# Where SP waits for the store: behind both closing barriers, on a semaphore that the closing clear does not touch

## The chip, the cores and the metric

One core of a Trainium2 chip. The metric is device microseconds of one execution; lower is better. The experiments ran on three chips, each beside the kernel before on the same chip. All runs in this text are fast: at full granted clock, and none over 1.5% above the fastest of its kernel. The core has five instruction queues: SP (issues most transfers here), ACT (ScalarE), DVE (VectorE), POOL (GpSimd) and PE (TensorE, which computes nothing in this kernel but takes part in every barrier).

A semaphore is a counter on which the queues wait for each other. Two kinds of instruction recur below: an EventSemaphore waits on a semaphore, changes it, or both; a DRAIN stands where a queue closes a piece of its work, and can wait on a semaphore and change one as well. In a barrier of the closing block every other queue counts itself in ("gather"), and goes on when POOL has seen all of them and counts up a second semaphore ("release").

"After the store's issue" below means: counted from the start of the last transfer that SP issues, the one that writes the result. Such times to the nanosecond are from the traces' records of instructions and of semaphore events; the printed views round to a tenth or a hundredth of a microsecond.

## The reference

```python
batch, dim = 1024, 4096          # x, y: float32
def reference(x, y, axis):       # axis = -1
    return np.sum(np.abs(x - y), axis=axis).astype(np.float32)
```

The kernel reads 33.5 MB and writes 4 KB.

## The kernel before

Each partition holds 8 rows. VectorE subtracts, ScalarE takes absolute values and sums, the last row goes in five pieces. What matters here is the end: the sums `ro` go out in one store, and SP's wait for that store is put ahead of the closing block which the framework adds to every kernel. In this cut, whose comments are added, `put` places an instruction in the program, and `s_end` counts the partial results.

```python
class Entry:
    ...
    def at_end(self, emit):
        nc = self.nc
        hook = nc.inst_callbacks[-1]
        here = nc.cur_bb.bb.name
        done = []

        def closing(ins):                    # called for each instruction that is added
            if done or nc.cur_bb.bb.name == here or ins.engine != mybir.EngineType.SP:
                return
            done.append(ins)
            emit()                           # at the first SP instruction of the closing block
        ...

    s_end = tc.alloc_semaphore("s_end")
    s_out = tc.alloc_semaphore("s_out")
    ...
    put(lambda: nc.sync.wait_ge(s_end, n_part + 3))
    put(lambda: nc.sync.dma_start(out=orr, in_=ro).then_inc(s_out, 16))
    entry.at_end(lambda: nc.sync.wait_ge(s_out, 16))
```

The closing block itself, as the built program has it (shortened: each barrier has a DRAIN and an EventSemaphore for each of PE, ACT, DVE and SP):

```
SP    DRAIN            waits for s_out (before the change)
each  DRAIN            joins barrier 1: counts up "gather"
POOL  EventSemaphore   waits for all of "gather";  POOL EventSemaphore: counts up "release"
each  EventSemaphore   waits for "release"
POOL  clears the range of semaphores 99 to 112 (the kernel's own)
each  DRAIN            joins barrier 2, and so on as in barrier 1
```

## Time and profile before

| | before |
|---|---|
| time, median of all 6 runs beside the changed kernel | 85.35 us |
| time of the profiled run | 85.36 us |
| its span (first to last instruction of the kernel) | 83.57 us |
| time less span | 1.79 us |
| store's issue starts | 81.346 us into the span |
| sixteenth increment of `s_out` | 1.447 us after it |
| SP's and PE's last instruction end | 2.180 and 2.225 us after it |

To read it: everything up to the store's issue is loads and arithmetic, and the change touches none of it. Left are 2.2 us of the span and 1.8 us outside the span (the records do not say how much of these lies ahead of the first instruction). The page's chain of waits does not show this part at all: it is followed back from the last instruction of a computing engine, and ends with VectorE's last sum at 81.32. Only the view of SP's own waits and the listing of the closing line's instructions do; the prediction shows both.

### The profile page before, as it was taken

The page shows a single profiled execution, that of the slowest core. Times are in us where ns is not written, and L with a number is a line of the kernel's source. Part 1 is how long each engine was busy: PE and PEld are TensorE (multiplying, and loading weights), DVE is VectorE, ACT ScalarE, POOL GpSimd, SP SyncE. Part 2 cuts the span into 40 slices and gives each one's busy share as a digit, 9 for nine tenths or more (in the row PEclk, how much of TensorE's full clock was granted, in tenths as well). Part 3 has the DMA queues.
Part 4 walks back from the last instruction along what each step waited for, and adds up shares of the span by engine and source line. Part 5 has one row for each costly group of instructions (what it writes and reads, how often), then busy time and mean ns, then how long its engine had stood idle before and what let it go on. Part 6 is the DMA issues. An engine that isn't in the chain of part 4 may idle for free.

```text
span 83.6 us, 103 instructions
## 1 busy us (share of the span) xinstructions
DVE 36.3 (43%) x16; ACT 31.6 (38%) x27; POOL 0.2 (0%) x4
## 2 busy tenths in 40 slices
DVE  0000000000000000000399999999099898997870
ACT  3200000000000000000002979697980899999960
POOL 0000000000000000000000000000000000000000
DMA  5991992992998899888889988889999999999910
GB/s 125 627 627 71 557 627 125 502 627 125 502 502 376 376 588 541 376 376 376 376 376 659 471 376 376 376 376 416 447 392 463 416 447 379 414 410 410 394 55 2
DMA packets 2592, 33.56 MB, mean 402 GB/s; under 512 B 416, under 2 KB 928, under 8 KB 1696
## 3 DMA queue, kind: packets, MB, share of 16 engines
q1 hardware_dynamic: 2448, 25.17, 71.6%
q10 hardware_dynamic: 144, 8.39, 23.2%
HBM read 33.55 MB, written 0.00 MB: 402 GB/s over the span
## 4 chain that ended last, share of the span: by engine, by line
DMA 68%; DVE 22%; ACT 7%; ACTq 0%; SPq 0%; issue 0%
DMA xa_rows<-in_x_dram 49%; DMA yb_rows<-in_y_dram 19%; DVE xa_rows L123 16%; ACT xb_rows L128 7%; DVE xb_rows L123 5%; DVE ro_sums L159 1%; ACTq L195 0%; SPq L102 0%
## 5 line engine op out<-in xcount | busy, mean ns | idle before, releaser
L123 DVE TENSOR_TENSOR xa_rows<-xa_rows,yb_rows 128x4096 f32<-128x4096 f32 x4 | 17.4, 4421 | 41.1 <-DMA xa_rows<-in_x_dram 41.1
L128 ACT ACTIVATE xa_rows<-xa_rows 128x4096 f32<-128x4096 f32 x4 | 14.5, 3617 | 44.9 <-DVE xa_rows L123 44.9
L123 DVE TENSOR_TENSOR xb_rows<-xb_rows,yb_rows 128x2048 f32<-128x2048 f32 (+5 forms) x9 | 17.9, 2019 | 3.6 <-DMA yb_rows<-in_y_dram 3.5
L128 ACT ACTIVATE xb_rows<-xb_rows 128x2048 f32<-128x2048 f32 (+5 forms) x9 | 15.2, 1686 | 3.1 <-DVE xb_rows L123 3.0
L128 ACT ACT_TABLE_LOAD x1 | 1.3, 1283 | 1.3 <-PEq L181 1.3
L128 ACT ACTIVATION_READ_ACCUMULATOR xb_rows<-xb_rows 128x1 f32 x9 | 1.7, 186 | 0.0
L128 ACT ACTIVATION_READ_ACCUMULATOR xa_rows<-xa_rows 128x1 f32 x4 | 0.7, 187 | 0.0
L157 DVE TENSOR_TENSOR last_piece<-xb_rows,yb_rows 128x288 f32<-128x288 f32 x1 | 0.5, 459 | 0.2 <-DMA yb_rows<-in_y_dram 0.2
L159 DVE TENSOR_REDUCE ro_sums<-last_piece 128x1 f32<-128x292 f32 x1 | 0.5, 458 | 0.1
L151 DVE TENSOR_REDUCE ro_sums<-half_sums 128x2 f32<-128x4 f32 x1 | 0.1, 149 | 0.0
L181 POOL MEMSET const-bfloat16-1.0<- 128x1 bf16 x1 | 0.1, 102 | 0.0
L181 POOL MEMSET const-uint8-127<- 128x1 uint8 x1 | 0.1, 102 | 0.0
L181 POOL MEMSET const-float32-1.0<- 128x1 f32 x1 | 0.1, 99 | 0.0
L181 POOL MEMSET const-float32-0.0<- 128x1 f32 x1 | 0.1, 98 | 0.2 <-issue 0.2
## 6 DMA issues: line engine op xcount, KB each, us to landing
xa_rows<-in_x_dram SPq DMA_DIRECT2D x1, 6144.0 KB, 40.6
xb_rows<-in_x_dram SPq DMA_DIRECT2D x1, 6144.0 KB, 54.3
yb_rows<-in_y_dram SPq DMA_DIRECT2D x3, 2048.0 KB, 15.5
xa_rows<-in_x_dram SPq DMA_DIRECT2D x1, 2048.0 KB, 24.1
xb_rows<-in_x_dram SPq DMA_DIRECT2D x1, 864.0 KB, 17.8
yb_rows<-in_y_dram SPq DMA_DIRECT2D x1, 864.0 KB, 16.0
xb_rows<-in_x_dram SPq DMA_DIRECT2D x1, 528.0 KB, 16.9
yb_rows<-in_y_dram SPq DMA_DIRECT2D x1, 528.0 KB, 17.7
```

Of the source, the lines that this page charges most:

```text
L123: put(lambda: nc.vector.tensor_sub(out=tx, in0=tx, in1=ty).then_inc(s_sub, 1))
L128: put(lambda: nc.scalar.activation(tx, tx, ABS, accum_out=to).then_inc(sem, 1))
L151: put(lambda: nc.vector.reduce_sum(out=ro[:, K - 3:K - 1], in_=half, axis=AX).then_inc(s_end, 1))
L157: put(lambda: nc.vector.tensor_sub(out=last[:, n_part:n_part + w], in0=tx, in1=ty).then_inc(s_end, 1))
L159: put(lambda: nc.vector.reduce_sum(out=ro[:, K - 1:K], in_=last, axis=AX, apply_absolute_value=True).then_inc(s_end, 1))
L181: nc = _bacc.Bacc("TRN2", target_bir_lowering=False, num_devices=1)
```

## The change

The intent: SP needs to hold the program open until the store has landed, but nobody else needs to wait for that. If SP waits behind the barriers, the barriers can run while the store is in flight. The first barrier is followed by POOL's clearing of the kernel's semaphores; a count that is still arriving must not be cleared, so `s_out` is now allocated outside of the kernel's range (the clear covers 99 to 111) and SP counts it back to zero itself.

```diff
-            if done or nc.cur_bb.bb.name == here or ins.engine != mybir.EngineType.SP:
+            if done or nc.cur_bb.bb.name == here or ins.engine != mybir.EngineType.Pool:
+                return
+            mine = [x.opcode for x in nc.cur_bb.bb.instructions if x.engine == mybir.EngineType.SP]
+            if mine.count("EventSemaphore") < 2:
                 return
...
-    s_out = tc.alloc_semaphore("s_out")
+    s_out = nc.alloc_semaphore("s_out")
...
-    entry.at_end(lambda: nc.sync.wait_ge(s_out, 16))
+    entry.at_end(lambda: nc.sync.wait_ge(s_out, 16).then_inc(s_out, -16))
```

In the built program this is one wait less on SP's first closing DRAIN (which stays) and one EventSemaphore more as SP's last instruction.

## The prediction

> **What bounds the kernel now.** All times below are microseconds from the span's start unless marked ns; starts to the nanosecond are from the trace's records of instructions and semaphore events, where the views round to a tenth.
>
> I read the page's head and its chain first, to see how much of the kernel the change can touch at all.
>
> ```profile
> span 83.6 us, 103 instructions
> DVE 36.3 (43%) x16; ACT 31.6 (38%) x27; POOL 0.2 (0%) x4
> DMA 68%; DVE 22%; ACT 7%; ACTq 0%; SPq 0%; issue 0%
> ```
>
> Two thirds of the chain are loads; no compute engine is busy half of the time. The body is bound by 33.55 MB at 402 GB/s and by the tail of the last pieces, and the change has no instruction there. It can only win after the last reduction. The timeline of the last microseconds shows where that begins:
>
> ```profile
> 80.86 0.46 DVE L159 TENSOR_REDUCE ro_sums<-last_piece 128x1 f32<-128x292 f32 x1
> 81.35 0.35 SPq L163 DMA_DIRECT2D out_dram<-ro_sums  x1
> ```
>
> The last sum ends at 81.32, SP issues the store from 81.346 to 81.693, and the span ends at 83.57. So 2.2 us of the span follow the store's issue start, with no engine computing. The view of what SP's queue waited for, from 82 to 84, says what fills them:
>
> ```profile
> SPq L195 <- DMA out_dram<-ro_sums: 1.1, 1, 1.1
> SPq L195 <- PEq L195: 0.6, 2, 0.4
> ```
>
> First a wait of 1.1 for the store, then two waits of together 0.6 inside the closing barriers. The first is a wait for memory, the second for the other engines, and before the change they come one after the other. The listing of the closing line's instructions has the pieces:
>
> ```profile
> L195 POOLq EVENT_SEMAPHORE  x4: 17/17/17, 82.9 to 83.5; - x4
> L195 SPq DRAIN  x3: 7/7/7, 82.8 to 83.1; - x3
> L195 SPq EVENT_SEMAPHORE  x2: 17/17/17, 83.0 to 83.5; - x2
> L195 PEldq EVENT_SEMAPHORE  x2: 51/51/51, 83.0 to 83.5; - x2
> L195 POOLq EVENT_SEMAPHORE_RANGE_CLEAR  x1: 114/114/114, 83.2 to 83.2; - x1
> ```
>
> SP's first DRAIN carries the wait for the store and starts at 82.809. Then: SP's DRAIN of the first barrier at 82.870, GpSimd collects at 82.903 and releases at 82.981, SP passes at 83.023; second barrier: SP's DRAIN at 83.114, GpSimd's DRAIN at 83.062, its clearing of the semaphores at 83.167 for 114 ns, DRAIN at 83.310, collecting at 83.389, release at 83.467; SP's last instruction at 83.509 (ends 83.526), PE's last at 83.520, 51 ns, which is the end at 83.571.
>
> **What the Trainium skill says.**
> "DMA: Bandwidth & Descriptors", section "Anatomy of one DMA — SWDGE (gpsimd) path": a DMA's semaphore cannot be updated until the last byte is confirmed to have landed, and HBM is the slowest target. The store here is issued by SP and not by GpSimd, but the trace agrees in kind: its packets are on the engines from 82.19 to 82.39, and its 16 increments come from 82.593 to 82.793. So 0.4 us of its flight is confirmation; nothing in the change shortens it.
>
> "Perfetto Trace Analysis", section "Sequencer-only Instruction (DRAIN, etc)": such an instruction is shown only from the moment its semaphores are satisfied to its end; its waiting and the propagation of its update are not shown. The trace agrees: the DRAIN that waited over a microsecond is 7 ns long, and starts 16 ns after the sixteenth increment. So the new last instruction will look short as well, and its start is what to read.
>
> "Runtime: NRT & Kernel Launch", section "The ~15µs preamble/postamble breakdown": after the kernel the runtime runs a barrier over all engines and then resets semaphores. Its section "Semaphores 0–2 are reserved" names semaphore 2 as that barrier's. The trace has events of semaphore 2 from 83.806 to 84.330, nine of them, and the profiled run's time is 85.36 against a span of 83.57: 1.79 us lie outside the span. That barrier needs SP too, so SP's exit still counts.
>
> **The change part by part.**
> Removed: the wait on SP's first DRAIN. The DRAIN itself stays, without a wait. Added: one EventSemaphore on SP behind its last barrier instruction, which waits for the 16 and takes 16 off. In the built program the listing of instructions is otherwise the same, and the range that GpSimd clears ends one semaphore earlier (99 to 111 in place of 99 to 112), so the closing barriers cannot wipe a count that is still arriving. Taking 16 off restores zero. Two costs need sizing: when SP now gets through the barriers, and what its last wait adds.
>
> 1. SP is free at 81.693, when the store's issue ends. What a DRAIN right behind a DMA issue costs can be read from the opening, where SP issues two loads and then meets the first barrier:
>
> ```profile
> L181 SPq DRAIN  x1: 125/125/125, 0.9 to 0.9; - x1
> ```
>
> That issue ended at 0.850 and the DRAIN started at 0.904, 54 ns later, and lasted 125 ns. So here: 81.693 + 0.054 + 0.125 = 81.872. In that opening case megabytes were in flight for tens of microseconds more, so a DRAIN does not wait for its engine's transfers to land.
>
> 2. The next DRAIN, the first barrier's: before, it started 82.870 - 82.816 = 0.054 after the end of the one ahead. So 81.872 + 0.054 = 81.926.
>
> 3. Both barriers: before, from SP's barrier DRAIN to the end of SP's last instruction 83.526 - 82.870 = 0.656, and to PE's end 83.571 - 82.870 = 0.701. All other engines were long in the barrier (ACT's and DVE's DRAINs end at 80.86 and 81.37), so SP is the one it waits for and the same length applies: SP through at 82.582, PE at 82.627.
>
> 4. The store's flight is untouched: last increment at 82.793. SP is then already waiting, for about 0.21. The wait ends 16 ns later at 82.809 and the instruction takes the 17 ns that every EventSemaphore of SP takes: 82.826.
>
> The span thus ends at 82.83 in place of 83.571: 0.745 shorter. The 0.656 + 0.061 of barriers go under the store's 1.1 us, and the end moves from PE's to SP's last instruction. Of the whole time this is under 1%: the barriers were all that could be hidden.
>
> 5. The runtime's barrier behind it. SP leaves 83.526 - 82.826 = 0.70 earlier. If SP was what that barrier waited for, the time falls by 0.70. There is a bit more to be had: among the nine events of semaphore 2 the step from the second to the third is 0.205, whereas the same step in the runtime's opening barrier is 0.039, so some engine came about 0.17 late. If that is PE (last out, with the 51 ns instruction), it now comes well before SP and this goes as well: 0.70 + 0.17 = 0.87. I can't tell from the records which engine it is, so I take the middle, 0.78.
>
> Sum: 85.26 - 0.78 = 84.48 us, a ratio of about 1.009.
>
> **The rivals.**
> First, a DRAIN that does wait. If SP's DRAIN without a wait, right behind the store, stayed until the store had landed, nothing would be hidden, and the added EventSemaphore would cost its 17 ns plus some 50 ns of step: about 85.3. Against it: the 125 ns in the opening, with the loads still in flight. I give it 4%.
>
> Second, barriers that become the bound. If the two barriers took longer than the store's remaining flight, the end would be theirs plus SP's last instruction. The slack is 0.21 us on a chain of 0.89 (81.693 to 82.582), so they would have to be a quarter slower than before. For it: the barriers now run beside the store's completion, and GpSimd's clear takes 114 ns as it is. Against it: 4 KB and 16 semaphore writes in 0.2 us is little traffic. If it happened, the time would be 84.5 to 84.8.
>
> Third, the time behind the span gives some back. SP is now the only late engine at the runtime's barrier, and the part of that barrier or of SP's own way into it that used to lie beside PE's is exposed. Before, SP and PE left within 45 ns of each other, so at most about 0.05 to 0.1 could be lost: 84.5 to 84.7.
>
> Fourth, a gain over 2%. It would need 1.7 us, and from the store's issue to the span's end there are only 1.88 us, of which the 1.1 of the store's flight remain. I see no way to it.
>
> **Range and chances.** The mechanism gives 84.39 (0.87 off) to 84.56 (0.70 off). The three runs of before spread from 85.23 to 85.81, with two within 0.03, so a median may sit a few tenths high; the second and third rivals also push up. Downwards there is only a store that lands earlier, which nothing suggests. Range 84.2 to 84.9. A change over 2% in either direction is all but excluded by the sizes: faster 1%, within 2% 98%, slower 1%.
>
> **What would show each step right or wrong.** In the changed kernel's trace SP's two first closing DRAINs should start near 81.75 and 81.93 (steps 1 and 2; near 82.8 if a DRAIN waits for the store). GpSimd's clear should be near 82.2 and PE's last instruction should end near 82.63 (step 3). SP should have three closing EventSemaphores in place of two, the last starting at 82.81, 16 ns behind the sixteenth increment; the view of SP's waits should show a wait for the store of about 0.2 in place of 1.1; the store should still land 1.4 after its issue; the span should be 82.8 (step 4). Time less span should be 1.7 to 1.85 against 1.79; were it over 2, the third rival holds. The body, up to the last reduction at 80.86, should be the same; a difference there is the run's, not the change's. The prediction is wrong if the time is at or above 85.0 with an undisturbed body.

## The result, and the profile after

The changed kernel took 84.47 us median (84.33 to 84.97, 6 runs) against 85.35 us (85.23 to 85.81, 6 runs): a ratio of 0.9899, 95% interval 0.9868 to 0.9929. A ratio here is the mean time of one kernel's fast runs over that of the other's of the same rounds, so it is not quite the ratio of the medians. It is a real gain of about 0.9 us, within 2%.

The head of the page, then two rows of the timeline at its end, in microseconds from the span's start:

```profile
span 82.7 us, 104 instructions
```

```profile
80.77 0.46 DVE L163 TENSOR_REDUCE ro_sums<-last_piece 128x1 f32<-128x292 f32 x1
81.25 0.35 SPq L167 DMA_DIRECT2D out_dram<-ro_sums  x1
```

The body drew loads that were 0.09 us faster in this one execution (the store is issued at 81.25 against 81.35). That is not the change's, and has to be taken off before the tails are compared. What SP's queue waited for, from 81 to 84 (waits in total, how many, the longest):

```profile
SPq L167 <- DVE ro_sums L163: 12.0, 1, 12.0
SPq L199 <- PEq L199: 0.6, 2, 0.4
SPq L168 <- SPq L168: 0.2, 1, 0.2
```

The wait for the store was 1.1 us and is 0.2; the 0.6 inside the barriers is the same. Two warnings on reading this view. It gives the releaser of the last row as SP itself, because SP now also changes that semaphore (it counts it back); by the records the sixteenth increment came from the transfer at 82.698 and the instruction started 17 ns later. And "PEq" in the second row stands for the barrier's release, which every engine counts down: it is not PE that SP waited for.

The closing line's instructions (count, duration in ns as min/median/max, first and last start in us):

```profile
L199 POOLq EVENT_SEMAPHORE  x4: 17/17/17, 81.9 to 82.4; - x4
L199 SPq DRAIN  x3: 7/7/125, 81.7 to 82.1; - x3
L199 SPq EVENT_SEMAPHORE  x2: 17/17/17, 82.0 to 82.5; - x2
L199 PEldq EVENT_SEMAPHORE  x2: 51/51/51, 82.0 to 82.5; - x2
L199 POOLq EVENT_SEMAPHORE_RANGE_CLEAR  x1: 113/113/113, 82.1 to 82.1; - x1
```

and the new instruction:

```profile
L168 SPq EVENT_SEMAPHORE  x1: 17/17/17, 82.7 to 82.7; - x1
```

Against the listing of before, every start has moved from 82.8 and later to 81.7 and later, one of SP's DRAINs takes 125 ns in place of 7, and the clear lies at 82.1, ahead of the store's landing at 82.7. The span ends with SP's new instruction at 82.73.

So the span became 0.84 us shorter, of which 0.09 is the body: 0.75. But the time became 85.36 - 84.33 = 1.03 us shorter, and 1.03 - 0.09 = 0.94. Time less span fell from 1.79 to 1.60. That part the span does not explain, and the experiments are about it.

### The profile page after: what moved, and what is told of

It reads as the page before. It is cut to its first block, busy times and chain, and to the rows that moved or that the text cites. A ratio compares the mean times of both kernels' runs of the same rounds, so it can differ in the third digit from the quotient of the medians.

```text
span 82.7 us, 104 instructions
## 1 busy us (share of the span) xinstructions
DVE 36.3 (44%) x16; ACT 31.6 (38%) x27; POOL 0.2 (0%) x4
## 4 chain that ended last, share of the span: by engine, by line
DMA 68%; DVE 22%; ACT 7%; ACTq 0%; SPq 0%; issue 0%
DMA xa_rows<-in_x_dram 49%; DMA yb_rows<-in_y_dram 19%; DVE xa_rows L127 16%; ACT xb_rows L132 7%; DVE xb_rows L127 5%; DVE ro_sums L163 1%; ACTq L199 0%; SPq L106 0%
```

## The experiments

The records of semaphore events reach beyond the kernel's last instruction: two groups of nine events of semaphore 2 follow it, which the Trainium skill ("Runtime: NRT & Kernel Launch", "Semaphores 0–2 are reserved") names as the runtime's barrier. In every trace the second group begins 0.785 to 0.790 us after the last event of the first, so only the first is of interest here. Undisturbed, as in the last group ahead of the kernel, consecutive events are 0.023 to 0.113 us apart. Behind the kernel before, the third comes 0.205 us after the second, so some engine was late there.

**Theory:** the closing barriers run under the store's flight, and the time then moves with the exit of an engine that is late in the runtime's barrier, PE by my guess; SP's own exit has slack there. **Rival:** the time moves with the last exit of any engine, which is SP's, and the extra 0.2 us is chance. A second rival for the first part: the gain is from the DRAIN that no longer waits, or from the semaphore's place, and not from what is hidden.

The body varies by some tenths from execution to execution, so besides the time each run is told by its tail: the profiled run's time less the start of the store's issue in that run. The two profiled runs of the changed kernel agree in it within 0.01 us. The tail does follow the barrier: in all fourteen traces it is 1.020 to 1.034 us longer than the time from the store's issue to the ninth event. And it does not rest on the profiled runs alone. Time less span is, for every execution (the span to a tenth), 1.55 to 1.63 us in the changed kernel's ten, against 1.74 to 1.84 in the 33 of before.

| run | profiled time | store's issue | tail | SP's exit | PE's exit | POOL's exit | events 1 / 3 / 5 of semaphore 2 | median | ratio |
|---|---|---|---|---|---|---|---|---|---|
| before | 85.36 | 81.346 | 4.01 | 2.180 | 2.225 | 2.138 | 2.460 / 2.699 / 2.766 | 85.35 | |
| changed | 84.33 | 81.254 | 3.08 | 1.478 | 1.284 | 1.197 | 1.519 / 1.758 / 1.826 | 84.47 | 0.9899 |
| again (changed) | 84.32 | 81.252 | 3.07 | 1.483 | 1.283 | 1.196 | 1.518 / 1.757 / 1.825 | 84.34 | 0.9886 |
| sem_only | 85.51 | 81.417 | 4.09 | 2.255 | 2.300 | 2.213 | 2.535 / 2.774 / 2.842 | 85.44 | 1.0032 |
| between | 84.91 | 81.374 | 3.54 | 1.705 | 1.751 | 1.664 | 1.986 / 2.225 / 2.292 | 84.89 | 0.9938 |
| on_pe | 84.48 | 81.295 | 3.19 | 1.237 | 1.528 | 1.195 | 1.807 / 1.880 / 1.947 | 84.56 | 0.9903 |
| late4 | 84.38 | 81.307 | 3.07 | 1.703 | 1.283 | 1.195 | 1.518 / 1.757 / 1.824 | 84.34 | 0.9872 |
| late10 | 84.71 | 81.385 | 3.33 | 2.018 | 1.282 | 1.195 | 1.517 / 1.756 / 2.139 | 84.73 | 0.9924 |
| on_act | 84.35 | 81.283 | 3.07 | 1.237 | 1.283 | 1.195 | 1.517 / 1.757 / 1.823 | 84.53 | 0.9889 |
| on_dve | 84.37 | 81.305 | 3.07 | 1.237 | 1.282 | 1.195 | 1.517 / 1.756 / 1.824 | 84.40 | 0.9877 |
| on_pool | 84.97 | 81.365 | 3.61 | 1.769 | 1.814 | 1.727 | 2.049 / 2.288 / 2.356 | 84.97 | 0.9935 |
| on_pool_last | 84.76 | 81.389 | 3.37 | 1.236 | 1.282 | 1.490 | 1.516 / 2.051 / 2.119 | 84.79 | 0.9957 |
| early | 84.03 | 81.231 | 2.80 | 1.481 | 0.737 | 0.650 | 0.972 / 1.211 / 1.610 | 84.10 | 0.9848 |
| early2 (same) | 84.70 | 81.902 | 2.80 | 1.480 | 0.737 | 0.650 | 0.972 / 1.211 / 1.609 | 84.43 | 0.9896 |

All in microseconds; exits and events are counted from the store's issue. Every kernel gave the right result.

**1. between: the wait stands between the two barriers.** In the edit, the hook fires one EventSemaphore earlier.

```diff
-            if mine.count("EventSemaphore") < 2:
+            if mine.count("EventSemaphore") < 1:
```

> SP's wait stands between the two closing barriers. Theory (barriers hide under the store's flight, time moves with the end of PE's last instruction): only the first barrier is hidden. SP's wait ends at 82.83 as counted in the trace of before, its second DRAIN comes 0.054 later, GpSimd collects after 0.033, releases after 0.078, PE passes after 0.053 and takes 0.051: PE ends at 83.10 against 83.57, so the time falls by about 0.47 us, a ratio of 0.9945. Rival (the gain is that the DRAIN behind the store no longer waits, wherever the wait goes): as the changed kernel, 0.86 us, 0.990.

What SP's queue waited for, 81 to 84:

```profile
SPq L168 <- SPq L168: 0.7, 1, 0.7
SPq L199 <- PEq L199: 0.3, 2, 0.2
```

The wait for the store was 0.7 us, so one barrier's worth was hidden and not two. The tail fell by 4.01 - 3.54 = 0.47 us, as the theory said, and the median is 84.89. The rival, under which any place behind the first DRAIN does as well, falls. This run does not tell PE from POOL: both left 0.474 us earlier than before.

**2. sem_only: the semaphore's place and the count back alone, the wait as before.** The edit is against the kernel before.

```diff
-    s_out = tc.alloc_semaphore("s_out")
+    s_out = nc.alloc_semaphore("s_out")
...
-    entry.at_end(lambda: nc.sync.wait_ge(s_out, 16))
+    entry.at_end(lambda: nc.sync.wait_ge(s_out, 16).then_inc(s_out, -16))
```

> The semaphore outside of the cleared range and the count back alone, with the wait where before has it: ahead of both barriers. Both theories: nothing is hidden, and counting back makes an EventSemaphore of its own ahead of the DRAIN, so 0.06 us more than before: ratio 1.000 to 1.001, span 83.6. Were the gain due to the semaphore's place, 0.990.

The tail grew by 0.08 us (4.09 against 4.01), somewhat over the 0.06 expected: the wait now is an instruction of its own ahead of the DRAIN. The ratio 1.0032 has an interval of 0.9997 to 1.0067. The semaphore's place gains nothing by itself; it is what makes the move safe.

**3. late4 and late10: SP leaves later still.** Idle DRAINs on SP behind its last wait.

```diff
-    entry.at_end(lambda: nc.sync.wait_ge(s_out, 16).then_inc(s_out, -16))
+    def ending():
+        nc.sync.wait_ge(s_out, 16).then_inc(s_out, -16)
+        for _ in range(4):                   # 10 in late10
+            nc.sync.drain()
+
+    entry.at_end(ending)
```

> As the changed kernel, with four idle DRAINs on SP behind the wait, 0.06 us each: SP leaves 0.24 us later, the span is 0.24 longer. Theory (SP's exit has slack in the runtime's barrier): the time stays within 0.1 us of the changed kernel's, ratio 0.990 to 0.991; time less span falls from 1.6 to about 1.4. Rival (the time moves with the last exit): 0.24 us more than the changed kernel, ratio 0.993.

> Ten such DRAINs: SP leaves 0.61 us later than in the changed kernel. Theory: the slack, at most about 0.35 us by the events of semaphore 2, is used up, and the rest is seen: 0.25 to 0.5 us over the changed kernel, ratio 0.993 to 0.996. Rival (last exit): 0.61 over it, ratio 0.997. If the slack is larger than thought, no change, 0.990.

The heads of the two pages, of late4 and of late10:

```profile
span 83.0 us, 108 instructions
```

```profile
span 83.4 us, 114 instructions
```

With four DRAINs SP leaves 0.225 us later than in the changed kernel (1.703 against 1.478), the span grows by as much, and the tail does not move: 3.07. The rival, by which the time follows the last exit, falls. With ten, SP leaves 0.54 us later (I had expected 0.61; each DRAIN of the series added 0.054) and the tail grows by 0.25. The events say why: SP is the engine of the fifth event, which follows SP's exit by 2.139 - 2.018 = 0.121 us. In the changed kernel that event comes at 1.826 anyhow, so SP may leave as late as 1.705 and has a slack of 0.227 us. Late4 used up 0.225 of it. Late10 overran it by 0.31, and the fifth event moved by 0.31; the tail grew by a little less, since the step from the fifth event to the sixth shrank from 0.098 to 0.043 us when SP was the late one.

**4. The last wait on each of the other engines.** If SP is not what the time follows, which engine is? The edit is one word, for PE, ScalarE and VectorE:

```diff
-    entry.at_end(lambda: nc.sync.wait_ge(s_out, 16).then_inc(s_out, -16))
+    entry.at_end(lambda: nc.tensor.wait_ge(s_out, 16).then_inc(s_out, -16))    # on_pe
```

> As the changed kernel, but PE has the last wait in place of SP. Theory (the runtime's barrier behind the kernel opens 0.235 us after PE's exit, and SP's exit has slack there): PE ends at about 0.05 behind the store, some 0.23 us later than in the changed kernel, and all of it is seen: about 0.70 us under before, ratio 0.992. Rival (the time moves with whichever engine leaves last, so SP's 17 ns or PE's 51 ns is all the difference): as the changed kernel within 0.04 us, ratio 0.990. In the trace: first event of semaphore 2 at 0.235 after PE's end either way by the theory.

> As the changed kernel, but ScalarE has the last wait. If ScalarE is the third engine (third event 0.515 after its exit): third event at 1.99 in place of 1.76, 0.23 us more than the changed kernel, ratio 0.992. If it is not, 0.989.

> As the changed kernel, but VectorE has the last wait. If VectorE is the third engine (third event 0.504 after its exit): third event at 1.99 in place of 1.76, 0.23 us more than the changed kernel, ratio 0.992. If it is not, 0.989.

On PE the tail grew by 0.11 us, half of the theory's 0.23 and more than the rival's 0.04, so both were off. The first event did wait for PE: it moved from 1.519 to 1.807. But the third moved only from 1.758 to 1.880, since the hold-up between the second and the third was gone (0.039 apart now, and 0.205 before). PE opens the runtime's barrier, and another engine, the third, is later than PE. My guess of PE as the late one falls here.

On ScalarE the second event moved by 0.07, to 1.626, and the third not at all: ScalarE is second and has slack. On VectorE no event moved.

**5. on_pool and on_pool_last.** GpSimd remained as the third engine. The first try had a slip: the hook fires when GpSimd's own part of the second barrier is about to be added, so the wait landed ahead of it.

> As the changed kernel, but GpSimd has the last wait. In the changed kernel the third event of semaphore 2 comes 0.561 us after GpSimd's exit. If GpSimd is that third engine, it now leaves at 1.48 after the store's issue in place of 1.20 and the third event comes at 2.04 in place of 1.76: 0.28 us more than the changed kernel, ratio 0.992. If it is not, nothing or little changes: 0.989.

The tail grew by 0.53 us and all engines left late, because the second barrier itself waited for the store; SP's queue shows that in its barrier waits:

```profile
SPq L199 <- PEq L199: 1.1, 2, 0.9
```

That says nothing on the question. The mended kernel adds the wait after the closing block is complete:

```diff
-    entry.at_end(lambda: nc.sync.wait_ge(s_out, 16).then_inc(s_out, -16))
+    return s_out
...
     with _tile.TileContext(nc) as tc:
-        tile_sub_abs_sum_kernel(tc, *args)
+        s_out = tile_sub_abs_sum_kernel(tc, *args)
+    nc.gpsimd.wait_ge(s_out, 16).then_inc(s_out, -16)
```

> Run on_pool had the wait ahead of GpSimd's part of the second barrier, by a slip; here it is GpSimd's last instruction, behind both. Theory (the order of semaphore 2 is PE, ScalarE, GpSimd, VectorE, SP, and GpSimd is late in it): GpSimd leaves at 1.48 after the store's issue, the third event of semaphore 2 comes at 2.04 in place of 1.76, and the time is 0.28 us over the changed kernel, ratio 0.993. Rival (VectorE is third and GpSimd is not late): as the changed kernel, 0.990.

GpSimd left 0.29 us later than in the changed kernel (1.490 against 1.197), the third event moved by 0.29 (2.051 against 1.758), and the tail by 0.30. This is the engine that the time follows: the third event comes 0.561 us after GpSimd's exit before (2.699 - 2.138), in the changed kernel (1.758 - 1.197) and here (2.051 - 1.490). The ratio, 0.9957, is above the 0.993 expected because one of the four runs took 85.5; the other three took 84.76 to 84.79.

The order PE, ScalarE, GpSimd and SP at the first, second, third and fifth event is shown by these runs. That VectorE is the fourth is by elimination. What GpSimd does in its 0.56 us is not in the records, and stays open.

**6. early and early2: a version meant to beat both.** If GpSimd's exit sets the time and SP has slack, the barriers should start sooner. In the changed kernel they cannot start before SP has issued the store (0.35 us) and has gone through a 0.125 us DRAIN behind it. Here SP joins the first barrier beforehand, and issues the store between joining and being released. The cut shows the new lines and leaves out those that they replace.

```diff
+    def store():                             # ahead of SP's first EventSemaphore of the closing block
+        nc.sync.wait_ge(s_end, n_part + 3)
+        nc.sync.dma_start(out=orr, in_=ro).then_inc(s_out, 16)
+
+    entry.inside(store)
...
-    s_end = tc.alloc_semaphore("s_end")      # within the cleared range
+    s_end = nc.alloc_semaphore("s_end")      # outside, as SP may read it beside the clear
...
+    def ending():
+        nc.sync.wait_ge(s_end, n_part + 3).then_inc(s_end, -(n_part + 3))
+        nc.sync.wait_ge(s_out, 16).then_inc(s_out, -16)
```

(`inside` is a hook like `at_end` which fires at SP's first EventSemaphore of the closing block; the count in `at_end`'s hook becomes 3.)

> A version meant to beat both: SP joins the first closing barrier before it issues the store (the wait for the last sum and the store stand between its DRAIN and its EventSemaphore), so the barriers start when DVE comes, not after the store's issue. Theory as the runs so far have it (the runtime's barrier takes its fifth event from SP, 0.12 us after SP's exit, and in the changed kernel the third event comes from an engine that is late by more than SP): the barriers end some 0.5 us earlier, SP's exit becomes the bound, the fifth event of semaphore 2 comes at 1.60 after the store's issue in place of 1.83, and the time falls by a further 0.2 us against the changed kernel; against before a ratio of 0.986. Rival (the barriers are hidden already, so starting them earlier gives nothing): as the changed kernel, 0.989. The span should be as the changed kernel's, 82.7 to 82.8.

> The changed kernel once more, unedited, as the yardstick beside the next runs on the same chip: ratio 0.990 against before.

> The version of run early once more beside the changed kernel on the same chip. Theory: 0.27 us under the changed kernel (in the profiled runs, time less the start of the store's issue was 2.80 against 3.08), a ratio of about 0.986 to 0.987 against before. Rival (the lower median of run early was the run's): the same as the changed kernel, 0.990.

SP's waits in run early, 81 to 84:

```profile
SPq L185 <- DVE ro_sums L180: 11.8, 1, 11.8
SPq L191 <- SPq L191: 0.7, 1, 0.7
SPq L224 <- PEq L224: 0.2, 1, 0.2
```

Only 0.2 us of waiting in barriers is left, and the wait for the store has grown back to 0.7: SP is through the barriers that much earlier. All engines but SP leave some 0.55 us earlier, SP's exit becomes the bound (fifth event at 1.61, 0.129 after it), and the tail is 2.80 in both, against 3.08. So the tail is 0.27 us shorter: 0.22 from the earlier fifth event, as expected ahead of run early, and 0.05 from the shorter step behind it that late10 had shown.

The record of every execution bears the tail out. In both versions the span ends with SP's wait, 1.48 us after the store's issue, so time less span compares the tails: it is 1.28 to 1.36 us in all twelve executions of this version, and 1.55 to 1.63 in all ten of the changed kernel.

The medians are less clear, because of the body. The first gave 84.10; the second, beside the changed kernel on the same chip, 84.43 against 84.34. In the second profiled run the body was slow, which these two views show (the timeline's end of early2, then of early):

```profile
81.42 0.46 DVE L180 TENSOR_REDUCE ro_sums<-last_piece 128x1 f32<-128x292 f32 x1
```

```profile
80.75 0.46 DVE L180 TENSOR_REDUCE ro_sums<-last_piece 128x1 f32<-128x292 f32 x1
```

The same last sum of the same kernel starts 0.67 us later. SP's own timeline shows where the two executions part (early2, then early):

```profile
61.27 2.87 SPq L135 DMA_DIRECT2D yb_rows<-in_y_dram  x1
```

```profile
61.27 2.18 SPq L135 DMA_DIRECT2D yb_rows<-in_y_dram  x1
```

One issue of a load took 0.69 us more. It lies nearly 9 us ahead of SP's first closing DRAIN (70.0 us in early2), from where on SP's instructions stand in another order than in the changed kernel. Executions with such a slow body occur in other kernels here too (before ran up to 85.90, sem_only up to 86.23), but in early2 four of six spans were 83.1 or more, while the changed kernel's four beside it were 82.7 to 82.9. Whether the version draws them more often or this was chance is not settled by the runs at hand. It has the better tail, by 0.27 us, and is not shown to be the better kernel in its median.

## Why the prediction was right

The time was put at 84.48 and measured at 84.47; the range 84.2 to 84.9 held it, with 98% on "within 2%". (The prediction's ratio of 1.009 is before over after; the measured ratio is the other way round.) An agreement of 0.01 us is luck, as told below; steps 1 to 4 are not. Step by step, taking off the 0.09 us of body in the profiled pair:

- Step 1, SP free and its first DRAIN: predicted to start 0.054 us after the issue and to last 125 ns. Measured 0.057 and 125. The opening's DRAIN was the right model, and the first rival (a DRAIN that waits for the store) is refuted: it ended at 81.784 while the store landed at 82.698.
- Step 2, the next DRAIN 0.054 later: measured 0.054.
- Step 3, both barriers in 0.656 to SP's last and 0.701 to PE's: measured 0.654 and 0.700. The second rival (barriers slowed by the store beside them) falls.
- Step 4, the store untouched and SP's wait about 0.21: the sixteenth increment came 1.444 us after the issue against 1.447, SP waited 0.206. The span was predicted at 82.826, which less the body's 0.092 is 82.734; measured 82.732.
- Step 5, the runtime's barrier, was mis-sized. It reckoned 0.70 us if SP was what that barrier waited for, 0.87 if PE was late in it, and took 0.78. The tail fell by 4.01 - 3.08 = 0.94. SP is not what it waits for (late4), and the late engine is not PE but GpSimd (on_pe, on_pool_last), whose exit moved from 2.138 to 1.197, by 0.941. So everything that the barriers gained is seen, including what SP's own last wait takes up at the end of the span, since that lies in SP's slack. The expected time less span of 1.7 to 1.85 was wrong for the same reason: 1.60. The third rival (some of the gain given back behind the span) had the sign wrong. The bound under the fourth was too tight: of the 1.88 us behind the store's issue, less 1.1 of flight, some 0.78 could be won at most, but what counts is POOL's exit and not the span's end, and 0.94 was won.

That the time came out within 0.01 us is two errors that cancel. The sum started from 85.26, the median of the three runs of before that the prediction had; the six beside the changed kernel gave 85.35, 0.09 more. And by these medians the gain was 85.35 - 84.47 = 0.88 and not 0.78. The two ratios measured for the changed kernel, 0.9899 and 0.9886, are 0.86 and 0.97 us of 85.3, on either side of the tail's 0.94; the body's spread does not allow more.

Two readings in the prediction need a word. It counts nine events of semaphore 2 behind the kernel; there are eighteen, and it read the first group, which is the one that moves. And it calls the 0.4 us between the store's last packet and its last increment confirmation: the trace shows the gap (82.391 to 82.793), and not what fills it.

## What to carry to other kernels

Closing work that needs nothing from the last store can run under its flight: put the wait for it behind that work, on a semaphore that the closing work does not clear. Judge such a change by the tail, not by the span or the chain of waits: the span ended with SP's wait, and yet SP could leave 0.23 us later at no cost, while 0.29 us of GpSimd cost 0.30. When the gain is below the body's spread, compare the distance from a fixed instruction to the end, which repeated here within 0.01 us.

## What the Trainium skill lacked or had wrong

- "Runtime: NRT & Kernel Launch", "The ~15µs preamble/postamble breakdown": it gives the barrier's total and a time for each hop (44 ns), which the undisturbed events bear out roughly (eight steps in 0.371 us ahead of the kernel). It lacks the order of the engines and how long each takes from its last instruction to its place: PE first, 0.234 to 0.235 us (0.279 in on_pe); ScalarE second, 0.145; GpSimd third, 0.561; SP fifth, 0.121 to 0.129. The long one sets when this kernel's barrier can close.
- The same section gives about 1.5 us for the barrier behind the kernel. Here, behind the kernel before, its nine events took 0.52 us, from 0.24 us after PE's exit.
- "Perfetto Trace Analysis", "Sequencer-only Instruction (DRAIN, etc)": no page has what a DRAIN costs right behind a transfer's issue. On SP it took 123 to 125 ns, 56 ns with one EventSemaphore between (run early), and 7 ns further on. In each of the first two cases it ended 0.179 to 0.182 us after the end of the issue, and it did not wait for the transfer to land.
- "DMA: Bandwidth & Descriptors", "Anatomy of one DMA — SWDGE (gpsimd) path": the fixed cost of about 2.0 us is for transfers issued by GpSimd. The 4 KB store issued by SP landed 1.443 to 1.450 us after the start of its issue in all fourteen traces; for transfers issued by SP the page has a first-byte latency, and no figure from issue to landing.
